# Layer kernel: the small tiles' pool ahead of the weights' pool, and a turn of seven buffers over two rings in the FFNs

## Chip, cores and metric

One core of a Trainium2 chip runs the whole kernel. The metric is the device time of one execution in microseconds, the median of three runs; lower is better. Engines: TensorE (PE in the profile; PEld is its weight load), VectorE (DVE), ScalarE (ACT), GpSimd (POOL) and SyncE (SP), which issues most of the DMAs.

## The reference

One layer of a streaming encoder on a batch of 1 with T = 256 tokens of width D = 2048, all in f32. What matters here are its two feed-forward networks (FFN1 and FFN2), with F = 5632:

```python
def swiglu(h, w_gate, w_up, w_down):
    return (jax.nn.silu(h @ w_gate) * (h @ w_up)) @ w_down

x = x + 0.5 * swiglu(rms_norm(x, ffn1_norm[i]), ffn1_w_gate[i], ffn1_w_up[i], ffn1_w_down[i])
...
x = x + mixed @ w_out[i]
x = x + 0.5 * swiglu(rms_norm(x, ffn2_norm[i]), ffn2_w_gate[i], ffn2_w_up[i], ffn2_w_down[i])
gate = jax.nn.sigmoid(rms_norm(x, ple_norm[i]) @ w_ple_gate[i])
e = (p[i] @ w_ple_proj[i]) * gate
x = x + rms_norm(e, ple_post_norm[i])
```

Between the two FFNs stands the mix (an S5 state-space group and a stick-breaking attention group with a common input and output projection); the last three lines are the last stage, the per-layer embedding.

## The kernel before

**Split matmuls.** TensorE multiplies in a rounded 32-bit format. So that the result keeps its precision, each 128x1024 half of a weight tile (two blocks of 128 rows, 512 columns) is split by `split` into hi, a rounded copy that ScalarE casts (L181), and lo, the rest, which VectorE subtracts (L184). Activations are split in the same way (nhi/nlo for a norm's output, hhi/hlo for the hidden layer and for sums). A product takes three matmuls of 128x512: hi·hi, hi·lo and lo·hi; the moving operand is the weight, the stationary one the activation. The lines are L305, L306 and L310 in `gemm_half`, and L480, L481 and L483 in `Seven.product`.

**Two ways through an FFN.** F is walked in NF = 11 column blocks of 512 for gate and up, then the down projection goes over four column blocks of D, two at a time. In blocks 0 to 6 of FFN1, beside which the preparation of S5 runs, and in block 0 of FFN2, the plain routines `gemm_block` and `gemm_pair` do the work. From block 7 of FFN1 (`early = 7`), from block 1 of FFN2 and in both down projections class `Seven` does it: some groups of four row blocks go as a `chunk`, in which sums and differences of weight blocks (VectorE, L487, tiles named sum) and of activations replace eight block products by seven, and the others as plain `column`s. A chunk calls `product` in the order 1, 5, 6, 4, 7, 2, 3.

**Where the split halves lie.** Pool `wts` has a ring of 5 for the raw weights (8,192 B per partition) and rings of 4 for whi and wlo (4,096 B each). Columns, `gemm_block`, `gemm_pair` and products 1, 2 and 3 take their halves from those. Products 5, 6, 4 and 7, made from sums, have a pool of their own, that of the phase `sums1` or `sums2`, with rings of 3 for shi and slo (beside 2 for the sums). Phases are pools that are opened and closed as the kernel goes on; they lie behind the fixed pools const, wts, act (split activations), com and small. Small holds 10 tiles of 32 B, thus 320 B per partition; wts, act and com are each a multiple of 2,048 B.

**The last stage.** `gemm_resident` multiplies with one code over three kinds of tiles: for the first quarters of the weight its halves lie in tiles of their own in a phase's pool (argument `own`), for the others in whi and wlo of wts; the stationary side is nhi/nlo (act), and for the small projection of the embedding pT, a tile of a phase's pool.

**What sets the order.** The code is written in one sequence; the framework orders each engine's instructions from it by its own estimate of what is ready, and a buffer of a ring can be written again when its last reader is done. `put_off` and `step` set where evictions and transposes stand. The raw weights are loaded on SP's queue, 1 MB a tile.

Of the kernel before, what the change touches and what calls it, by code (L numbers as in the profile page):

```python
# [2 lines left out]

# [7 lines left out]
F32R = mybir.dt.float32r  # L11
# [5 lines left out]
P = 128  # L17
# [9 lines left out]
NB = 512  # L27
# [6 lines left out]
def layer_kernel(ctx: ExitStack, tc: tile.TileContext, a: dict, shapes: dict, out: bass.AP):  # L34
# [15 lines left out]
    assert TT == 2 and NP == 64 and HC == 16 and DH == P and NC == 64 and SW == NH * DH  # L50

    cpool = ctx.enter_context(tc.tile_pool(name="const", bufs=1))
    wp = ctx.enter_context(tc.tile_pool(name="wts", bufs=4))
    actp = ctx.enter_context(tc.tile_pool(name="act", bufs=1))
    comp = ctx.enter_context(tc.tile_pool(name="com", bufs=1))
    smp = ctx.enter_context(tc.tile_pool(name="small", bufs=10))
    dramp = ctx.enter_context(tc.tile_pool(name="scratch", bufs=1, space=bass.MemoryType.DRAM))
    accp = ctx.enter_context(tc.tile_pool(name="acc", bufs=4, space=bass.MemoryType.PSUM))
    auxp = ctx.enter_context(tc.tile_pool(name="aux", bufs=2, space=bass.MemoryType.PSUM))
# [3 lines left out]
    def uid(s):  # L63
        count[0] += 1
        return f"{s}_{count[0]}"
# [7 lines left out]
    def phase(name):  # L73
        return tc.tile_pool(name=name, bufs=1, reuse_waits="tile")
# [24 lines left out]
    def step():  # L99
        for g in list(beside):  # L100
            if next(g, beside) is beside:
                beside.remove(g)

    def finish(g):
        for _ in g:
            pass
# [71 lines left out]
    def split(hi, lo, src, scale=None, pinned=False):  # L178

        if scale is None:  # L180
            copy = nc.scalar.copy(hi, src)  # L181
            if pinned:
                pin(copy)
            nc.vector.tensor_tensor(out=lo, in0=src, in1=hi.bitcast(F32), op=ALU.subtract)  # L184
        else:
            split_each(hi.unsqueeze(1), lo.unsqueeze(1), src.unsqueeze(1), [scale])
# [63 lines left out]
    def first_quarters(w, xn):  # L250
# [28 lines left out]
        xn.parted(1, second.rearrange("p (j s) -> p j s", j=4))  # L279
        return [(h, *parts[h]) for h in range(2)], weight_split(raws[1], 4)  # L280

    def weight_split(raw, nk, own=None):
        for h in range(nk // 2):
            if own:
                hi, lo = (own.tile([P, 2, NB], F32R, name=uid(s)) for s in ("whi", "wlo"))
            else:
                hi, lo = (wp.tile([P, 2, NB], F32R, tag=s, name=uid(s)) for s in ("whi", "wlo"))
            split(hi, lo, raw[:, 2 * h : 2 * h + 2, :])
            yield h, hi, lo

# [141 lines left out]
    def sum_forms(pool, u, kind="n"):  # L432

        sums = pool.tile([P, 2, NB], F32, tag="sum", name=uid("rows"), bufs=2)
        s = sums.rearrange("p j n -> p (j n)").rearrange("p (z j x b) -> p z j x b", z=4, j=2, b=32)
        (a11, a21), (a12, a22) = ([u[:, k : k + 2, 4 * t : 4 * t + 4] for t in range(TT)] for k in (0, 2))
        for z, (x, y, op) in enumerate((
            (a21, a22, ALU.subtract), (s[:, 0], a11, ALU.subtract),
            (a11, a21, ALU.subtract), (a12, s[:, 1], ALU.add),
        )):  # L440
            nc.vector.tensor_tensor(out=s[:, z], in0=x, in1=y, op=op)
        both = halves(kind)
        split(*both, sums.rearrange("p j n -> p (j n)").rearrange("p (z t) -> p z t", z=4))
        return both

    class Seven:
# [20 lines left out]
            self.begun.add(z)  # L467
            return fresh

        def product(self, z, left, src, own, final):  # L470
            hi, lo = (
                (self.pool if own else wp).tile([P, 2, NB], F32R, tag=s, name=uid(s), bufs=3 if own else None)
                for s in (("shi", "slo") if own else ("whi", "wlo"))
            )
            split(hi, lo, src)
            ps = self.bank(z)
            begin = self.begin(z)
            lh, ll = left
            for j in range(2):
                nc.tensor.matmul(ps, lhsT=lh[j], rhs=hi[:, j], start=begin and j == 0, stop=False)  # L480
                nc.tensor.matmul(ps, lhsT=ll[j], rhs=hi[:, j], start=False, stop=False)  # L481
            for j in range(2):
                nc.tensor.matmul(ps, lhsT=lh[j], rhs=lo[:, j], start=False, stop=z in final and j == 1)  # L483
# [6 lines left out]
        def chunk(self, kb, final=()):  # L490

            raws = []
            for w, n0 in self.ws:
                raw = wp.tile([P, 4, NB], F32, tag="raw", name=uid("raw"), bufs=5)
                nc.sync.dma_start(
                    raw, w[4 * kb * P : 4 * (kb + 1) * P, n0 : n0 + NB].rearrange("(j p) n -> p j n", p=P)
                )
                raws.append(raw)
            b11, b21, b12, b22 = (raw[:, 2 * h : 2 * h + 2, :] for raw in raws for h in range(2))
            parts, sums = self.act(kb), self.sums(kb)  # L500

            def whole(k, t):
                return [[u[:, 2 * k + j, t * P : (t + 1) * P] for j in range(2)] for u in parts]

            def summed(z):
                return [[u[:, z, j * P : (j + 1) * P] for j in range(2)] for u in sums]

            self.product(1, whole(0, 0), b11, False, final)
            t1 = self.add(b11, b12)
            self.product(5, summed(0), t1, True, final)  # L510
            step()
            t2 = self.add(t1, b22)
            self.product(6, summed(1), t2, True, final)
            t4 = self.add(t2, b21)
            self.product(4, whole(1, 1), t4, True, final)
            step()
            t3 = self.add(b12, b22)
            self.product(7, summed(2), t3, True, final)
            self.product(2, whole(1, 0), b21, False, final)
            step()  # L520
            self.product(3, summed(3), b22, False, final)
            step()

        def column(self, side, kbs, final=False):
# [14 lines left out]
    def ffn(i, xn, nxt, bg=None):  # L539
        wg, wu, wd = (a[f"ffn{i}_w_{s}"][0] for s in ("gate", "up", "down"))  # L540
        hT = []
        pools = ExitStack()
        early = 7 if bg else 0
        sevens = None if bg else pools.enter_context(phase(f"sums{i}"))
        hp = pools.enter_context(phase(f"h{i}"))
        side = ExitStack()
        prep = bg(side) if bg else None
# [15 lines left out]
        for f in range(NF):  # L563
            if prep and f == early:
                finish(prep)
                side.close()
                prep = None
                sevens = pools.enter_context(phase(f"sums{i}"))
                hp = pools.enter_context(phase(f"h{i}b"))
                sums = [sum_forms(sevens, whole_rows(sevens, xn(kb)), "h") for kb in range(2)]  # L570
            if sevens and f:
# [17 lines left out]
                s = Seven(xn, lambda kb: sums[kb], ((wg, f * NB), (wu, f * NB)), sevens)  # L589
# [32 lines left out]
            if f == 0 and not bg:  # L622
                both = gemm_pair(xn, ((wg, 0), (wu, 0)), KD)
                pg = next(both)
                sums = [sum_forms(sevens, whole_rows(sevens, xn(kb))) for kb in range(2)]
# [51 lines left out]
        for n in range(0, ND, 2):  # L677
# [14 lines left out]
            s = Seven(kept, lambda kb: sum_forms(sevens, rows(kb)), ((wd, n * NB), (wd, (n + 1) * NB)), sevens)  # L692
            plan = plans[n // 2]
            left = sum(u[0] == "s" for u in plan)
            for u in plan:
                kb, final = int(u[1:]), u == plan[-1]
# [715 lines left out]
    pool = s5p.enter_context(phase("s5"))  # L1412
# [10 lines left out]
    pool = atp.enter_context(phase("attn"))  # L1423
# [93 lines left out]
    s = small(1)  # L1517
# [144 lines left out]
```

## Time and profile before

| | |
|---|---|
| median of 3 runs | 1852.08 us (1851.85 to 1852.86) |
| the profiled execution | 1852.7 us, span 1850.6 us |
| TensorE busy | 1838.3 us, granted clock 1.0 |
| VectorE busy | 1460.6 us |
| ScalarE busy | 1027.4 us |
| GpSimd busy | 63.3 us |
| HBM read | 373.46 MB |

All of these but the median are of the one profiled execution. Its stages begin at (us): FFN1's blocks 0 to 6 at 0, blocks 7 to 10 at 316.29, FFN1's down projection near 478, the mix at 724.40, FFN2's block 0 near 1035, its blocks 1 to 10 at 1089.91, its down projection at 1506.75, the last stage at 1742.38. Stage by stage, the busy time of PE, PEld, DVE, ACT and POOL in windows cut near such times:

```profile
116.00:294.00 178.00, 178.00 (x1026) 146.46 (x1025) 115.62 (x127) 74.83 (x84) 21.78 (x41) 1.00 0.81 253
478.00:724.20 246.20, 245.88 (x1081) 202.29 (x1081) 196.25 (x197) 141.32 (x158) 2.52 (x4) 1.00 0.61 209
724.20:1035.00 310.80, 309.35 (x2080) 260.09 (x2079) 218.07 (x271) 191.07 (x249) 25.96 (x32) 1.00 0.62 204
1506.70:1742.20 235.50, 235.50 (x1039) 194.69 (x1039) 188.21 (x190) 137.46 (x152) 0.00 (x0) 1.00 0.62 210
```

The columns are the window, its length, the busy time of the five engines with the number of instructions, the granted clock, the DMA share and GB/s. In a row of the timeline stand the start, the duration, the engine, line and operation, what it writes and reads, and in brackets idle time just before it with the instruction that ended it. TensorE overlaps matmuls: the distance from one start to the next, and not the duration, says what one costs.

### The profile page before, as it was taken

What the parts mean: (1) busy time and instruction counts of PE and PEld (TensorE: products, weight loads), DVE (VectorE), ACT (ScalarE), POOL (GpSimd) and SP (SyncE); (2) the same over time, 40 slices, a digit from 0 to 9 for tenths busy, and PEclk for the clock granted to TensorE, in tenths of its full rate; (3) what the DMA queues carried; (4) which work ended last, traced back from release to release, by engine and by line L of the source; (5) the groups of instructions that cost most, each with busy time, mean ns of one, the idle gap of its engine ahead of it and who ended that gap; (6) DMA issues with size and microseconds to landing.
All of it is one profiled execution on the core that took longest, in us unless ns stands there. A gap on an engine that the chain in (4) does not pass through costs nothing.

```text
span 1850.6 us, 23946 instructions
## 1 busy us (share of the span) xinstructions
PE 1838.3 (99%) x9032; PEld 1518.5 (82%) x9032; DVE 1460.6 (79%) x1718; ACT 1027.4 (56%) x1187; POOL 63.3 (3%) x108
## 2 busy tenths in 40 slices
PE   9999999999999999999999999999999999999998
PEld 7888888778888888888897888888888888888887
DVE  8967665998888876687567798989898978887665
ACT  7444443655564656365685565655555555565654
POOL 0011000000000000010021000000000000000000
PEclk9999999999999999999999999999999999999999
DMA  9888868566756567675646776665656675666663
GB/s 334 281 274 277 252 217 246 173 228 200 241 196 213 192 217 248 190 262 166 216 142 218 224 262 216 235 206 198 218 198 219 207 244 185 223 195 217 208 219 125
DMA packets 232307, 406.36 MB, mean 220 GB/s; under 512 B 26784, under 2 KB 50720, under 8 KB 231904
## 3 DMA queue, kind: packets, MB, share of 16 engines
q1 hardware_dynamic: 227824, 392.81, 63.8%
q0 software_dynamic: 3648, 10.62, 1.8%
q8 instruction: 70, 1.15, 0.2%
q10 hardware_dynamic: 720, 1.41, 0.2%
q14 instruction: 45, 0.37, 0.1%
HBM read 373.46 MB, written 11.93 MB: 208 GB/s over the span
## 4 chain that ended last, share of the span: by engine, by line
PE 92%; DVE 3%; DMA 2%; ACT 2%; SPq 1%; issue 1%; DVEq 0%; ACTq 0%
PE acc L305 18%; PE acc L310 18%; PE acc L306 18%; PE aux L305 7%; PE aux L306 7%; PE aux L310 7%; PE acc L480 3%; PE acc L481 2%; PE acc L483 2%; PE aux L480 2%; PE aux L483 2%; PE aux L481 2%; DVE wlo L184 1%; SPq L1170 1%; DMA raw<-in_w_in 1%
## 5 line engine op out<-in xcount | busy, mean ns | idle before, releaser
L181 ACT CAST whi<-raw 128x1024 fp32r<-128x1024 f32 x639 | 668.1, 1052 | 684.8 <-PE acc L306 388.9
L184 DVE TENSOR_TENSOR wlo<-raw,whi 128x1024 fp32r<-128x1024 f32 x639 | 772.0, 1221 | 297.9 <-ACT whi L181 295.1
L305 PE MATMUL acc<-whi,nhi 128*128 128x512 f32 x1232 | 482.9, 392 | 1.8 <-ACT whi L181 1.7
L306 PE MATMUL acc<-whi,nlo 128*128 128x512 f32 x1232 | 479.9, 390 | 0.0
L310 PE MATMUL acc<-wlo,nhi 128*128 128x512 f32 x1232 | 340.6, 389 | 0.2 <-DVE wlo L184 0.2
L305 PEld LDWEIGHTS acc<-whi,nhi 128*128 128x128 f32 x1232 | 231.5, 188 | 52.2 <-ACT whi L181 3.0
L310 PEld LDWEIGHTS acc<-wlo,nhi 128*128 128x128 f32 x1232 | 231.2, 188 | 48.8 <-DVE wlo L184 0.6
L306 PEld LDWEIGHTS acc<-whi,nlo 128*128 128x128 f32 x1232 | 231.6, 188 | 47.2
L306 PE MATMUL acc<-whi,hlo 128*128 128x512 f32 x376 | 146.4, 389 | 0.0
L305 PE MATMUL acc<-whi,hhi 128*128 128x512 f32 x376 | 146.3, 389 | 0.0
L181 ACT CAST shi<-sum 128x1024 fp32r<-128x1024 f32 x108 | 113.4, 1052 | 43.1 <-DVE sum L487 39.6
L306 PE MATMUL aux<-whi,hlo 128*128 128x512 f32 x344 | 133.8, 389 | 0.0
L305 PE MATMUL aux<-whi,hhi 128*128 128x512 f32 x344 | 133.8, 389 | 0.0
L184 DVE TENSOR_TENSOR slo<-sum,shi 128x1024 fp32r<-128x1024 f32 x108 | 130.9, 1216 | 0.6 <-ACT shi L181 0.5
L310 PE MATMUL acc<-wlo,hhi 128*128 128x512 f32 x376 | 114.6, 389 | 0.2 <-DVE wlo L184 0.2
L310 PE MATMUL aux<-wlo,hhi 128*128 128x512 f32 x344 | 106.0, 389 | 0.0
L306 PE MATMUL aux<-whi,nlo 128*128 128x512 f32 x240 | 93.4, 389 | 0.0
L305 PE MATMUL aux<-whi,nhi 128*128 128x512 f32 x240 | 93.4, 389 | 0.0
L306 PEld LDWEIGHTS acc<-whi,hlo 128*128 128x128 f32 x376 | 70.6, 188 | 15.1 <-DVE hlo L184 0.4
L310 PEld LDWEIGHTS acc<-wlo,hhi 128*128 128x128 f32 x376 | 70.5, 188 | 15.2 <-DVE wlo L184 0.6
L305 PEld LDWEIGHTS acc<-whi,hhi 128*128 128x128 f32 x376 | 70.6, 188 | 14.6
L306 PEld LDWEIGHTS aux<-whi,hlo 128*128 128x128 f32 x344 | 64.6, 188 | 13.5
(345 smaller groups left out, 2162.6 us busy)
## 6 DMA issues: line engine op xcount, KB each, us to landing
raw<-in_ffn_w_up SPq DMA_DIRECT2D x88, 1024.0 KB, 5.8
raw<-in_ffn_w_down SPq DMA_DIRECT2D x88, 1024.0 KB, 5.1
raw<-in_ffn_w_gate SPq DMA_DIRECT2D x86, 1024.0 KB, 6.2
raw<-in_w_in SPq DMA_DIRECT2D x32, 1024.0 KB, 5.7
raw<-in_w_out SPq DMA_DIRECT2D x16, 1024.0 KB, 5.3
raw<-in_w_ple_gate SPq DMA_DIRECT2D x16, 1024.0 KB, 5.1
hT<-mid SPq DMA_DIRECT2D x160, 64.0 KB, 3.5
h<-mid SPq DMA_DIRECT2D x176, 32.0 KB, 3.6
```

What stands on the lines that cost most here:

```text
L181: copy = nc.scalar.copy(hi, src)
L184: nc.vector.tensor_tensor(out=lo, in0=src, in1=hi.bitcast(F32), op=ALU.subtract)
L305: nc.tensor.matmul(ps[t], lhsT=lh, rhs=hi[:, j, cols], start=start and j == 0, stop=False)
L306: nc.tensor.matmul(ps[t], lhsT=ll, rhs=hi[:, j, cols], start=False, stop=False)
L310: nc.tensor.matmul(ps[t], lhsT=lh, rhs=lo[:, j, cols], start=False, stop=stop and j == 1)
L480: nc.tensor.matmul(ps, lhsT=lh[j], rhs=hi[:, j], start=begin and j == 0, stop=False)
L481: nc.tensor.matmul(ps, lhsT=ll[j], rhs=hi[:, j], start=False, stop=False)
L483: nc.tensor.matmul(ps, lhsT=lh[j], rhs=lo[:, j], start=False, stop=z in final and j == 1)
L1170: nc.sync.dma_start(zt[0][p1 : p1 + HC, z], sv[p0 : p0 + HC, r % 2 * 2 + r // 2])
```

## The change

Two edits. The pool small is made ahead of wts, so every tile of wts, act and com moves up by 320 B, and the phases' tiles stay where they were. And a new function `weight_pair` hands out the buffers for each split half: while a phase made by `sums_phase` is open, it counts the halves, and of every seven the second, fourth and sixth go to that phase's shi and slo (three deep), the others to whi and wlo of wts (four deep), whether they belong to a column, to `gemm_pair` or to a product. `product` loses its argument `own`, so a half's place no longer depends on whether it was made from a sum. Outside such a phase all halves take whi and wlo, as before. The loops, the number of matmuls, casts and subtractions and the arithmetic are the same.

```diff
@@ -50,10 +50,10 @@
     assert TT == 2 and NP == 64 and HC == 16 and DH == P and NC == 64 and SW == NH * DH
 
     cpool = ctx.enter_context(tc.tile_pool(name="const", bufs=1))
+    smp = ctx.enter_context(tc.tile_pool(name="small", bufs=10))
     wp = ctx.enter_context(tc.tile_pool(name="wts", bufs=4))
     actp = ctx.enter_context(tc.tile_pool(name="act", bufs=1))
     comp = ctx.enter_context(tc.tile_pool(name="com", bufs=1))
-    smp = ctx.enter_context(tc.tile_pool(name="small", bufs=10))
     dramp = ctx.enter_context(tc.tile_pool(name="scratch", bufs=1, space=bass.MemoryType.DRAM))
     accp = ctx.enter_context(tc.tile_pool(name="acc", bufs=4, space=bass.MemoryType.PSUM))
     auxp = ctx.enter_context(tc.tile_pool(name="aux", bufs=2, space=bass.MemoryType.PSUM))
@@ -279,12 +279,30 @@
         xn.parted(1, second.rearrange("p (j s) -> p j s", j=4))
         return [(h, *parts[h]) for h in range(2)], weight_split(raws[1], 4)
 
+    ring = [None, 0]
+
+    def weight_pair():
+
+        extra, i = ring
+        ring[1] += 1
+        pool, tags = (extra, ("shi", "slo")) if extra and i % 7 % 2 else (wp, ("whi", "wlo"))
+        return [
+            pool.tile([P, 2, NB], F32R, tag=s, name=uid(s), bufs=3 if pool is extra else None) for s in tags
+        ]
+
+    @contextmanager
+    def sums_phase(name):
+        with phase(name) as pool:
+            ring[:] = [pool, 0]
+            yield pool
+            ring[0] = None
+
     def weight_split(raw, nk, own=None):
         for h in range(nk // 2):
             if own:
                 hi, lo = (own.tile([P, 2, NB], F32R, name=uid(s)) for s in ("whi", "wlo"))
             else:
-                hi, lo = (wp.tile([P, 2, NB], F32R, tag=s, name=uid(s)) for s in ("whi", "wlo"))
+                hi, lo = weight_pair()
             split(hi, lo, raw[:, 2 * h : 2 * h + 2, :])
             yield h, hi, lo
 
@@ -467,11 +485,8 @@
             self.begun.add(z)
             return fresh
 
-        def product(self, z, left, src, own, final):
-            hi, lo = (
-                (self.pool if own else wp).tile([P, 2, NB], F32R, tag=s, name=uid(s), bufs=3 if own else None)
-                for s in (("shi", "slo") if own else ("whi", "wlo"))
-            )
+        def product(self, z, left, src, final):
+            hi, lo = weight_pair()
             split(hi, lo, src)
             ps = self.bank(z)
             begin = self.begin(z)
@@ -505,20 +520,20 @@
             def summed(z):
                 return [[u[:, z, j * P : (j + 1) * P] for j in range(2)] for u in sums]
 
-            self.product(1, whole(0, 0), b11, False, final)
+            self.product(1, whole(0, 0), b11, final)
             t1 = self.add(b11, b12)
-            self.product(5, summed(0), t1, True, final)
+            self.product(5, summed(0), t1, final)
             step()
             t2 = self.add(t1, b22)
-            self.product(6, summed(1), t2, True, final)
+            self.product(6, summed(1), t2, final)
             t4 = self.add(t2, b21)
-            self.product(4, whole(1, 1), t4, True, final)
+            self.product(4, whole(1, 1), t4, final)
             step()
             t3 = self.add(b12, b22)
-            self.product(7, summed(2), t3, True, final)
-            self.product(2, whole(1, 0), b21, False, final)
+            self.product(7, summed(2), t3, final)
+            self.product(2, whole(1, 0), b21, final)
             step()
-            self.product(3, summed(3), b22, False, final)
+            self.product(3, summed(3), b22, final)
             step()
 
         def column(self, side, kbs, final=False):
@@ -541,7 +556,7 @@
         hT = []
         pools = ExitStack()
         early = 7 if bg else 0
-        sevens = None if bg else pools.enter_context(phase(f"sums{i}"))
+        sevens = None if bg else pools.enter_context(sums_phase(f"sums{i}"))
         hp = pools.enter_context(phase(f"h{i}"))
         side = ExitStack()
         prep = bg(side) if bg else None
@@ -565,7 +580,7 @@
                 finish(prep)
                 side.close()
                 prep = None
-                sevens = pools.enter_context(phase(f"sums{i}"))
+                sevens = pools.enter_context(sums_phase(f"sums{i}"))
                 hp = pools.enter_context(phase(f"h{i}b"))
                 sums = [sum_forms(sevens, whole_rows(sevens, xn(kb)), "h") for kb in range(2)]
             if sevens and f:
```

The order within the queues changes in FFN1 from block 7 on and in FFN2. VectorE at the end of FFN1's block 6 and the start of block 7, before (wlo_448 and wlo_450 are the two halves of the first weight tile of block 7, wlo_455 and wlo_457 those of the second; h and mid are block 6's result, whole and rows make the sums of activations):

```order
L184 TENSOR_TENSOR wlo_448_2846<-raw_446_2843,whi_447_2845 128x1024
L184 TENSOR_TENSOR wlo_450_2850<-raw_446_2843,whi_449_2849 128x1024
L641 SCALAR_TENSOR_TENSOR h_435_2791<-acc_411_2625,sm_74_459,sg_410_2622 128x512
L641 SCALAR_TENSOR_TENSOR h_435_2791<-acc_412_2626,sm_74_459,sg_410_2622 128x512
L216 STREAM_TRANSPOSE mid_458_2901<-h_435_2791 128x4x4x32 x2
L184 TENSOR_TENSOR wlo_455_2882<-raw_453_2879,whi_454_2881 128x1024
L184 TENSOR_TENSOR wlo_457_2886<-raw_453_2879,whi_456_2885 128x1024
L426 TENSOR_TENSOR whole_436_2819<-nhi_16_143,nlo_17_144 128x1024
L441 TENSOR_TENSOR rows_437_2821<-whole_436_2819 128x256 x2
```

And in the changed kernel:

```order
L184 TENSOR_TENSOR wlo_448_2846<-raw_446_2843,whi_447_2845 128x1024
L656 SCALAR_TENSOR_TENSOR h_435_2791<-acc_411_2625,sm_74_459,sg_410_2622 128x512
L656 SCALAR_TENSOR_TENSOR h_435_2791<-acc_412_2626,sm_74_459,sg_410_2622 128x512
L216 STREAM_TRANSPOSE mid_458_2901<-h_435_2791 128x4x4x32 x2
L184 TENSOR_TENSOR wlo_455_2882<-raw_453_2879,whi_454_2881 128x1024
L444 TENSOR_TENSOR whole_436_2819<-nhi_16_143,nlo_17_144 128x1024
L184 TENSOR_TENSOR slo_450_2850<-raw_446_2843,shi_449_2849 128x1024
L459 TENSOR_TENSOR rows_437_2821<-whole_436_2819 128x256 x2
L459 TENSOR_TENSOR rows_437_2821<-rows_437_2821,whole_436_2819 128x256
L184 TENSOR_TENSOR slo_457_2886<-raw_453_2879,shi_456_2885 128x1024
```

The second half of the first tile, now slo_450, moved from a place ahead of h to one behind h, the transposes, wlo_455 and whole.

ScalarE in FFN2's block 9, within its second chunk, before (sum_2070 is the chunk's fourth sum, for product 7; 2073 and 2077 are the halves of its last two products, 2081 and 2083 those of the next weight tile, 2086 and 2088 those of the one behind it):

```order
L181 CAST shi_2067_11620<-sum_2066_11618 128x1024
L181 CAST whi_2081_11670<-raw_2080_11668 128x1024
L181 CAST whi_2083_11674<-raw_2080_11668 128x1024
L576 COPY sg_2051_11575<-acc_2057_11585 128x512
L181 CAST shi_2071_11633<-sum_2070_11631 128x1024
L181 CAST whi_2086_11707<-raw_2085_11705 128x1024
L181 CAST whi_2088_11711<-raw_2085_11705 128x1024
```

And in the changed kernel:

```order
L181 CAST shi_2067_11620<-sum_2066_11618 128x1024
L181 CAST shi_2073_11643<-raw_2053_11577 128x1024
L181 CAST shi_2083_11674<-raw_2080_11668 128x1024
L591 COPY sg_2051_11575<-acc_2057_11585 128x512
L181 CAST shi_2088_11711<-raw_2085_11705 128x1024
L181 CAST whi_2071_11633<-sum_2070_11631 128x1024
L181 CAST whi_2077_11657<-raw_2054_11579 128x1024
L181 CAST whi_2081_11670<-raw_2080_11668 128x1024
L181 CAST whi_2086_11707<-raw_2085_11705 128x1024
```

The cast for product 7, now whi_2071, stands behind the casts of 2073, 2083 and 2088, of which the last two belong to later weight tiles.

More of the change, by code (lines that the diff above doesn't have):

```diff
@@ L1 @@
 import math
-from contextlib import ExitStack
+from contextlib import ExitStack, contextmanager
 import concourse.bass as bass
```

## The prediction

> **What bounds the kernel now.** First the page: how busy the engines are, and the tenths of the span.
>
> ```profile
> PE 1838.3 (99%) x9032; PEld 1518.5 (82%) x9032; DVE 1460.6 (79%) x1718; ACT 1027.4 (56%) x1187; POOL 63.3 (3%) x108
> PE   9999999999999999999999999999999999999998
> PEclk9999999999999999999999999999999999999999
> ```
>
> TensorE is busy from end to end at the full granted clock, so only what holds up a matmul, or stretches it, can be won or lost. To see how much that is I took the start of the first matmul of each stage from the timeline of PE, and counted the program's matmuls between (the program has 8,536; the page's x9032 counts f32 ones several times). These rows begin: the up projection of FFN1's column block 6; block 7; the mix; FFN2's block 1; FFN2's down projection; and the last stage.
>
> ```profile
> 294.53 0.39 PE L305 MATMUL acc<-whi,nhi 128*128 128x512 f32 x1
> 316.29 0.39 PE L305 MATMUL acc<-whi,nhi 128*128 128x512 f32 x1
> 724.40 0.39 PE L305 MATMUL acc<-whi,nhi 128*128 128x512 f32 x1
> 1089.91 0.39 PE L480 MATMUL acc<-whi,hhi 128*128 128x512 f32 x1
> 1506.75 0.39 PE L305 MATMUL acc<-whi,hhi 128*128 128x512 f32 x1
> 1742.38 0.39 PE L305 MATMUL acc<-whi,nhi 128*128 128x512 f32 x1
> ```
>
> Between the first two lie 96 matmuls: 21.76 us, 226.7 ns from start to start (226.65 over longer quiet stretches). I call this the normal pitch. Where the change reaches: 316.29 to 724.40 has 1,770 matmuls, 408.11 us against 401.17 at the normal pitch, 6.94 over. FFN2's up part has 1,830: 416.84 against 414.77, 2.07 over. Its down part has 1,038: 235.63 against 235.26, 0.37 over. The mix keeps its order on every engine and is left out; FFN2's block 0, which lies between, runs at the normal pitch. So **9.4 us is all there is to win**, 0.5% of the time.
>
> Next, what the 9.4 us are. The timeline of PE shows the stops of FFN1.
>
> ```profile
> 336.29 0.62 PE L483 MATMUL acc<-slo,hhi 128*128 128x512 f32 x2
> 337.80 0.50 PE L480 MATMUL aux<-shi,hhi 128*128 128x512 f32 x1 [0.89 <-ACT shi L181]
> 338.15 0.39 PE L481 MATMUL aux<-shi,hlo 128*128 128x512 f32 x1
> ...
> 364.67 0.40 PE L481 MATMUL aux<-whi,hlo 128*128 128x512 f32 x1
> 366.04 0.50 PE L480 MATMUL acc<-shi,nhi 128*128 128x512 f32 x1 [0.97 <-ACT shi L181]
> 366.37 0.39 PE L481 MATMUL acc<-shi,nlo 128*128 128x512 f32 x1
> ...
> 407.28 0.62 PE L483 MATMUL aux<-wlo,hhi 128*128 128x512 f32 x2
> 409.56 0.50 PE L480 MATMUL acc<-shi,nhi 128*128 128x512 f32 x1 [1.67 <-ACT shi L181]
> 409.90 0.39 PE L481 MATMUL acc<-shi,nlo 128*128 128x512 f32 x1
> ...
> 632.72 0.40 PE L481 MATMUL aux<-shi,nlo 128*128 128x512 f32 x1
> 633.26 0.74 PE L483 MATMUL aux<-slo,nhi 128*128 128x512 f32 x2
> 633.84 0.39 PE L480 MATMUL acc<-whi,hhi 128*128 128x512 f32 x1
> ...
> 647.49 0.39 PE L305 MATMUL acc<-whi,hhi 128*128 128x512 f32 x1
> ...
> 649.59 0.39 PE L305 MATMUL acc<-whi,hhi 128*128 128x512 f32 x1
> ```
>
> A row of x2 has its second start a pitch later. The first three stops are steps that exceed the pitch by 1.2, 1.25 and 1.95 us (for the last: 407.51 to 409.90 is 2.39, two pitches are 0.45): **4.4 us**. The two below, in the down projection, are 0.44 and, over the six matmuls from 647.49 to 649.59, 0.74 us: **1.2 us**. FFN2 has only two steps of a tenth each. That leaves 9.38 − 4.36 − 1.18 − 0.23 = **3.6 us that are no stop at all**: matmuls a few ns too long, spread over the chunks. What these are, the last stage shows most cleanly, where one routine with one code runs over three kinds of tiles:
>
> ```profile
> 1813.29 0.40 PE L305 MATMUL acc<-whi,pT 128*128 128x512 f32 x1
> 1816.09 0.40 PE L305 MATMUL acc<-whi,nhi 128*128 128x512 f32 x1
> 1821.60 0.39 PE L305 MATMUL acc<-whi,nhi 128*128 128x512 f32 x1
> 1822.97 0.39 PE L305 MATMUL acc<-whi,nhi 128*128 128x512 f32 x1
> 1827.05 0.39 PE L305 MATMUL acc<-whi,pT 128*128 128x512 f32 x1
> ```
>
> Twelve matmuls whose stationary side (pT) lies in a phase's pool and whose moving side lies in the weights' pool: 2.80 us, 233.3 ns each. Then 24 with the moving side in the phase's pool and the stationary one in the activations' pool: 5.51 us, 229.6. Then both back in the old pools: the first six take 228.3 each, the next 18 take 4.08 us, 226.7. Instructions, types and shapes are the same: what differs is **where the tiles lie**. shi and slo lie in a phase's pool too, and in before every chunk goes back and forth.
>
> **What the change does to that.** Every pool between the weights' pool and the phases is a multiple of 2,048 B per partition but one: the small pool, 320 B. Before, a weights' or activations' tile and a phase's tile are therefore never a multiple of 2,048 B apart, always 320 B off; with the small pool in front of both, they always are. If the offset makes the matmuls long, the 3.6 us go, and some 0.2 in the last stage (24 × 3.0 ns, 12 × 6.7 ns, and six at 1.7): **−3.8 us**. If it is something else, nothing goes, or more comes (rivals). The two ends are thus −3.8 and a loss; I take −3.8, since the slow rows are all such 320 B pairs, or stand right behind one, and no steady pair at one residue is slow. Against it stands the row at 1827.05, from where on both sides lie in the phase's pool, at no offset: its first six matmuls again take 228 to 236 ns, no more than the six that also follow a return to normal. This is a reading of addresses against durations, not a thing that the trace shows by itself.
>
> *By the Trainium skill* ("TensorE: Matmul & The Clock Gate", section "Step-by-step: what each phase is for") TensorE has two independent read ports into SBUF, one for the streamed side and one for the weight load, and a load takes nothing from a running matmul. By that rule the place of one side against the other cannot matter and this term is 0; the steps of 229.6 and 233.3 against 226.7 ns do not agree with it.
>
> **The turn of seven.** It adds no instruction to VectorE, ScalarE or TensorE: the same casts and subtractions write other buffers. What it changes is which buffer must be free first, and so what may stand early in an engine's queue. A row of the waits (line waited for, us in total, times, longest), two windows, and VectorE's timeline at the start of block 7:
>
> ```profile
> ACT whi L181 <- PE acc L306: 388.9, 272, 3.0
> 316.30:478.00 161.70, 158.18 (x691) 129.24 (x690) 155.02 (x159) 90.56 (x94) 4.40 (x8) 1.00 0.65 213
> 1090.00:1506.70 416.70, 416.70 (x1831) 343.23 (x1830) 375.73 (x366) 228.57 (x236) 4.33 (x8) 1.00 0.66 216
> 316.27 1.41 DVE L641 SCALAR_TENSOR_TENSOR h<-acc,sm,sg 128x512 f32<-128x512 f32 x2 [3.81 <-PE acc L310]
> 317.59 1.30 DVE L216 STREAM_TRANSPOSE mid<-h 128x512 f32<-128x512 f32 x2
> 318.81 2.32 DVE L184 TENSOR_TENSOR wlo<-raw,whi 128x1024 fp32r<-128x1024 f32 x2
> 321.05 1.22 DVE L426 TENSOR_TENSOR whole<-nhi,nlo 128x1024 f32<-128x1024 f32 x1
> 322.30 0.76 DVE L441 TENSOR_TENSOR rows<-whole 128x256 f32<-128x256 f32 x2
> ```
>
> (The windows' columns are: length, then PE, PEld, DVE, ACT, POOL busy.) ScalarE waits 388.9 us for a buffer that PE releases, so a deeper ring does let it run ahead. But in FFN1's blocks 7 to 10 VectorE is busy 155.0 of 161.7 us, and its idle time lies ahead of 316.27: a deeper ring hides nothing that VectorE hasn't done. I went through both orders and gave each VectorE row its duration from such rows (1.13 us from start to start for 128x1024). Before, wlo_450 comes ahead of block 6's h, so it is there when PE needs it; now slo_450 stands behind two h rows, two transposes, wlo_455 and whole. In the rows above that is 316.27 to 318.81, plus 1.12, plus 1.25: it begins at 321.2 and ends near 322.3, while PE, at its pace of before, wants it 16 matmuls after 316.29, at 319.9. That is a **new stop of some 2.4 us** at 320, where there was none. Behind it VectorE's sum of work is the same, and the tally gives 3.3 to 3.7 us late by 340, and no more later, against 4.36 in three stops. I take **0** for blocks 7 to 10 (from −0.7, which the tally gives, to +1). If VectorE really had slack there, up to −4.4.
>
> FFN1's down projection: the two places are late because VectorE stands still shortly before, for lack of a free buffer, and then has too much at once.
>
> ```profile
> 613.77 1.23 DVE L184 TENSOR_TENSOR wlo<-raw,whi 128x1024 fp32r<-128x1024 f32 x1 [1.49 <-ACT whi L181]
> 616.49 1.23 DVE L184 TENSOR_TENSOR wlo<-raw,whi 128x1024 fp32r<-128x1024 f32 x1 [1.49 <-ACT whi L181]
> ```
>
> The turn lets it use those 3 us, more than the 1.2 that it is late: **−1.1**.
>
> FFN2's up part has 41 us of free VectorE time (375.7 of 416.7) and no stop, so it can only lose. In block 9 the order of ScalarE, shown with the change, puts shi_2088, for a later half, ahead of whi_2071, the next product's. shi_2088's buffer is released by the matmul that starts here:
>
> ```profile
> 1385.72 0.39 PE L481 MATMUL acc<-shi,hlo 128*128 128x512 f32 x1
> L181 ACT CAST shi<-sum 128x1024 fp32r<-128x1024 f32 x108 | 113.4, 1052 | 43.1 <-DVE sum L487 39.6 <-PE acc L481 2.7 <-issue 0.3
> ```
>
> whi_2071 is wanted 9 matmuls, 2.04 us, later; the matmul's own 0.39 and two casts of 1.05 make 2.49: **+0.45**. Behind it stand the casts of two later products, with 40 matmuls of room. A place like it on VectorE in block 10 (a wlo behind the h rows and transposes) comes to +0.6 by the same count. Together **+1.0** (0 to 1.3).
>
> Moving the small pool costs no instruction. On SP's queue the weight loads move up by some rows; S5's first load at the end of FFN1 now waits for a later matmul, but the weight load behind it waits for the same one as before: 0.
>
> **Sum**: −3.8 + 0 − 1.1 + 1.0 = −3.9 us. The profiled execution took 1852.7 us (1850.6 of it the span, 2.1 around it), 0.6 above the median of 1852.08, within the 1851.85 to 1852.86 of the runs; its parts are no different, so I take the sum off the median: **1848.2 us**, own range 1845.6 to 1850.5. A difference under 0.2% (3.7 us, so 1848.4 to 1855.8) counts here as no change: the forecast lies on that edge.
>
> **Rivals.**
>
> *A phase's pool is slow in itself* (slower). Its tiles lie behind all others, and if distance or place is what costs, the change spreads the cost: 4,878 matmuls stand in FFN phases (1,770 and 3,108), three of seven halves would take 229.6 ns and the other four, each right behind such a one, 228.3: 2,091 × 3.0 ns + 2,787 × 1.7 ns = 6.2 + 4.7 us. Less the 3.6 there now and the 0.1 of the turn: +7.2, **1859.3** (1856 to 1863). For it: the six at 1827.05, and that pT is slow too. Against it: 320 B separates the cases as well. It decides wherever shi and slo matmuls stay above 229 ns.
>
> *The place of a tile within 2,048 B is what costs*, and the phases' place is the bad one: then all 7,764 matmuls of split weights move to it, 7,764 × 3.0 = 23 us less 3.7: about **1871**. For it the same six; against it, that the weights' place would have been the good one by accident.
>
> *No effect of addresses at all* (no change): the long steps come from changing tiles of any sort. The sum is then −0.1, **1852.0** (1850.5 to 1853.5). This is also what the skill's rule would give. Against it: the 18 matmuls from 1822.97 change the weights' tile every six as well, at 226.7.
>
> *All stops go as well*: 9.4 + 0.2, **1842.5**, if VectorE's order were better than I read it; little speaks for it.
>
> **Chances.** Offset 0.60 (of that 0.35 below 1848.4); no effect 0.12; phase pool slow 0.18; place within 2,048 B 0.08; all stops gone 0.02. Faster 0.37, same 0.35, slower 0.28 (0.26 from the two, the rest from larger new stops). The range, 1845.6 to 1861.0, holds the forecast's own, the case of no effect and the better part of the slow pool.
>
> **What would show it.** Right: shi and slo rows of L480 at the pitch of 226.7 in FFN2; the 24 and the 12 matmuls of the last stage too; a stop near 320 us; none at 632 and 647; small ones in FFN2's blocks 9 and 10. Wrong: shi or slo at 229 or more (the pool), every matmul longer (the place), or stops of FFN1 gone by more than 1 us.

## The result and the profile after

| | before | changed |
|---|---|---|
| median | 1851.97 us (1851.40 to 1852.86, 22 runs) | 1849.71 us (1848.78 to 1850.29, 22 runs) |
| profiled execution's span | 1850.6 us | 1848.5 us |
| ratio | 1 | 0.9987 (95% interval 0.9981 to 0.9993) |

The change is 2.3 us faster, 0.13%. That is under the 0.2% that the prediction counts as a change, yet the interval lies clear of 1. Both profiled executions took 0.6 to 0.7 us more than these medians (1852.7 and 1850.29 us), so differences between the two profiles can be compared. The first row of the page and four windows, cut at the stages' first matmuls less a quarter of a microsecond (FFN1's blocks 7 to 10, its down projection, FFN2's blocks 1 to 10, its down projection; columns as before):

```profile
PE 1836.6 (99%) x9032; PEld 1519.8 (82%) x9032; DVE 1462.7 (79%) x1718; ACT 1019.6 (55%) x1187; POOL 62.1 (3%) x108
316.20:477.81 161.61, 159.17 (x691) 130.38 (x690) 156.44 (x157) 84.69 (x89) 4.38 (x8) 0.99 0.63 211
477.81:723.76 245.95, 245.12 (x1081) 202.75 (x1080) 197.44 (x200) 142.80 (x159) 0.00 (x0) 1.00 0.61 209
1089.39:1505.71 416.32, 415.81 (x1831) 343.13 (x1830) 378.89 (x368) 228.32 (x239) 4.33 (x8) 1.00 0.65 217
1505.71:1740.99 235.28, 235.28 (x1039) 194.93 (x1038) 187.06 (x189) 133.98 (x150) 0.00 (x0) 1.00 0.61 210
```

From first matmul to first matmul the four stages took 161.77, 246.34, 416.84 and 235.63 us before: every one is shorter, by 0.2 to 0.5 us. Those are small differences of larger ones. I took the steps from start to start of all 7,764 matmuls of split weights in each trace, and divided what exceeds 226.65 ns into **long matmuls** (steps under 0.3 us) and **stops** (the others; matmuls at half clock, further down, count among them). This table, in us, also has the experiments below; "long" is the sum over the FFN stages from 316 us on, with FFN2's block 0. Long matmuls and stops are from one profiled execution of each kernel, the median is of all its runs.

| kernel | long | stops, blocks 7 to 10 | stops, FFN1 down | stops, FFN2 | median |
|---|---|---|---|---|---|
| before | 3.64 | 4.36 | 1.16 | 0.23 | 1851.97 |
| changed | 0.60 | 4.90 | 1.10 | 1.36 | 1849.71 |
| e1, small pool in front only | 0.42 | 4.49 | 0.72 | 0.41 | 1848.83 |
| e2, turn of seven only | 17.41 | 4.59 | 0.00 | 1.08 | 1866.04 |
| e3, 512 B off | 0.60 | 4.97 | 0.49 | 1.33 | 1849.44 |
| e4, turn starts at 6 | 1.04 | 3.98 | 0.00 | 2.26 | 1849.43 |
| e5, best of both | 0.49 | 4.01 | 0.00 | 0.41 | 1847.42 |
| e6, 128 B off | 15.67 | 4.49 | 0.22 | 1.07 | 1864.89 |
| e7, 448 B off | 18.22 | 4.50 | 0.11 | 1.08 | 1867.06 |
| e8, small pool between | 28.97 | 4.14 | 0.00 | 0.22 | 1892.71 |
| e9, 256 B off | 0.65 | 4.88 | 0.53 | 1.33 | 1849.68 |
| e10, 64 B off | 17.42 | 4.59 | 0.52 | 1.07 | 1865.55 |

Between before and changed, the long matmuls fell by 3.0 us and the stops grew by 1.6. The last stage shows the long ones best, at the same instructions as in the prediction (PE's timeline of the changed kernel: first the twelve with pT, then both kinds of weights' tiles, then pT again):

```profile
1811.95 0.39 PE L323 MATMUL acc<-whi,pT 128*128 128x512 f32 x1
1814.67 0.39 PE L323 MATMUL acc<-whi,nhi 128*128 128x512 f32 x1
1825.55 0.39 PE L323 MATMUL acc<-whi,pT 128*128 128x512 f32 x1
```

The twelve take 2.72 us, 226.7 ns each instead of 233.3; the next 48, of both kinds, 10.88 us, 226.7 each. Where the tiles lie no longer tells.

The stop at 320 us came as forecast. PE's timeline, and VectorE's ahead of it:

```profile
319.83 0.39 PE L324 MATMUL acc<-shi,nlo 128*128 128x512 f32 x1
322.46 0.73 PE L328 MATMUL acc<-slo,nhi 128*128 128x512 f32 x2 [2.24 <-DVE slo L184]
...
323.99 0.63 PE L324 MATMUL acc<-shi,nlo 128*128 128x512 f32 x1
324.41 1.06 PE L328 MATMUL acc<-slo,nhi 128*128 128x512 f32 x2
325.26 0.63 PE L323 MATMUL acc<-whi,nhi 128*128 128x512 f32 x1
```

```profile
316.41 1.41 DVE L656 SCALAR_TENSOR_TENSOR h<-acc,sm,sg 128x512 f32<-128x512 f32 x2 [6.54 <-PE acc L328]
317.73 1.30 DVE L216 STREAM_TRANSPOSE mid<-h 128x512 f32<-128x512 f32 x2
318.95 1.18 DVE L184 TENSOR_TENSOR wlo<-raw,whi 128x1024 fp32r<-128x1024 f32 x1
320.06 1.22 DVE L444 TENSOR_TENSOR whole<-nhi,nlo 128x1024 f32<-128x1024 f32 x1
321.19 1.22 DVE L184 TENSOR_TENSOR slo<-raw,shi 128x1024 fp32r<-128x1024 f32 x1
```

slo begins at 321.19 behind just the rows that the order put ahead of it, and the step is 2.63 us, 2.40 over the pitch. Not forecast is what follows: the steps from 323.99 on are 0.42 to 0.43 us, half speed, until 326.6. A window over it has the granted clock in its third column from the right:

```profile
323.00:326.70 3.70, 3.70 (x11) 2.88 (x10) 3.70 (x6) 1.78 (x2) 0.00 (x0) 0.55 0.86 284
```

The second thing not forecast lies at the end of FFN1's down projection. PE, then ScalarE and SP's queue:

```profile
713.19 0.50 PE L324 MATMUL aux<-whi,hlo 128*128 128x512 f32 x1 [0.83 <-DVE hlo L184]
```

```profile
703.55 1.06 ACT L181 CAST shi<-raw 128x1024 fp32r<-128x1024 f32 x1 [0.72 <-PE aux L324]
709.69 1.05 ACT L181 CAST whi<-raw 128x1024 fp32r<-128x1024 f32 x1 [5.08 <-DMA raw<-in_w_in]
710.64 1.05 ACT L181 CAST hhi<-hT 128x1024 fp32r<-128x1024 f32 x1
```

```profile
694.38 8.91 SPq L229 DMA_DIRECT2D h<-mid  x12
703.39 0.53 SPq L313 DMA_DIRECT2D raw<-in_w_in  x1
```

The cast of the mix's first weight (in_w_in) now stands ahead of an hhi that FFN1 still needs. Its load was issued at 703.39, behind twelve DMAs that turn blocks, and landed six microseconds later. The kernel before issued it later still, at 705.76, but there no cast that waited for it stood in front of an hhi. ScalarE waited 5.1 us with hhi behind; hlo and the matmul came 1.1 us late. The two old stops of the down projection, at 632 and 647, have gone.

FFN2's stops are the two that were forecast, in block 9 and block 10:

```profile
1386.58 0.51 PE L495 MATMUL aux<-whi,nhi 128*128 128x512 f32 x1 [0.30 <-ACT whi L181]
...
1474.98 0.73 PE L328 MATMUL acc<-wlo,hhi 128*128 128x512 f32 x2 [0.21 <-DVE wlo L184]
```

### The profile page after: what moved, and what is told of

Its sections match the earlier page's. It is cut to its first block, busy times and chain, and to the rows that moved or that the text cites. A ratio compares the mean times of both kernels' runs of the same rounds, so it can differ in the third digit from the quotient of the medians.

```text
span 1848.5 us, 23966 instructions
## 1 busy us (share of the span) xinstructions
PE 1836.6 (99%) x9032; PEld 1519.8 (82%) x9032; DVE 1462.7 (79%) x1718; ACT 1019.6 (55%) x1187; POOL 62.1 (3%) x108
## 5 line engine op out<-in xcount | busy, mean ns | idle before, releaser
L184 DVE TENSOR_TENSOR wlo<-raw,whi 128x1024 fp32r<-128x1024 f32 x473 | 573.2, 1224 | 214.1 <-ACT whi L181 206.5
L181 ACT CAST whi<-raw 128x1024 fp32r<-128x1024 f32 x473 | 491.4, 1050 | 398.3 <-PE acc L324 258.0
L184 DVE TENSOR_TENSOR slo<-raw,shi 128x1024 fp32r<-128x1024 f32 x166 | 202.5, 1220 | 43.8 <-ACT shi L181 43.6
L181 ACT CAST shi<-raw 128x1024 fp32r<-128x1024 f32 x166 | 174.3, 1051 | 113.4 <-PE acc L324 32.7
L181 ACT CAST whi<-sum 128x1024 fp32r<-128x1024 f32 x61 | 64.2, 1052 | 96.1 <-DVE sum L502 80.8
L181 ACT CAST shi<-sum 128x1024 fp32r<-128x1024 f32 x47 | 49.5, 1052 | 74.4 <-DVE sum L502 62.4
L324 PE MATMUL acc<-whi,hlo 128*128 128x512 f32 x216 | 84.1, 389 | 0.0
L184 DVE TENSOR_TENSOR wlo<-sum,whi 128x1024 fp32r<-128x1024 f32 x61 | 74.6, 1222 | 1.9 <-ACT whi L181 1.2
L184 DVE TENSOR_TENSOR hlo<-hT,hhi 128x1024 fp32r<-128x1024 f32 x56 | 68.3, 1219 | 4.8 <-ACT hhi L181 4.5
L502 DVE TENSOR_TENSOR sum<-sum,raw 128x1024 f32<-128x1024 f32 x54 | 66.0, 1222 | 1.0
```

Source lines behind the costliest of these rows:

```text
L324: nc.tensor.matmul(ps[t], lhsT=ll, rhs=hi[:, j, cols], start=False, stop=False)
L502: nc.vector.tensor_tensor(out=t, in0=x, in1=y, op=ALU.add)
```

## The experiments

**The two edits apart.** e1 is the kernel before with this alone:

```diff
+    smp = ctx.enter_context(tc.tile_pool(name="small", bufs=10))
     wp = ctx.enter_context(tc.tile_pool(name="wts", bufs=4))
     actp = ctx.enter_context(tc.tile_pool(name="act", bufs=1))
     comp = ctx.enter_context(tc.tile_pool(name="com", bufs=1))
-    smp = ctx.enter_context(tc.tile_pool(name="small", bufs=10))
```

> Before with the small pool in front of the weights' pool and nothing else; every engine's order is that of before. Offset theory (matmuls are long when their two operands do not lie a multiple of 2,048 B apart, as by the 320 B of before): the 3.6 us of long matmuls in the FFN stages fall to about 0.6 as in the changed kernel, the stops stay at 4.4 + 1.2 us, the time is 3.2 to 3.6 us under before, near 1848.6. Rival (the turn of seven itself took the long matmuls away): nothing changes, 1852.0.

Measured: 1848.83 us, ratio 0.9983 (0.9974 to 0.9991). Long matmuls 3.64 to 0.42 with every engine's order unchanged. So the addresses did it, and the turn had no part in it.

e2 is the changed kernel with that line moved back behind com.

> The turn of seven alone, the small pool left behind the weights' pool; every engine's order is that of the changed kernel. Offset theory: three of seven halves of 4,878 matmuls lie 320 B off and run near 229.6 ns, the halves behind them near 228.3, some 8 to 11 us of long matmuls in the FFN stages: 1857 to 1861. Rival (the turn took the long matmuls away): as the changed kernel, 1849.7.

Measured: 1866.04 us, ratio 1.0074 (1.0061 to 1.0087): 14 us slower than before, and slower than either time expected. Long matmuls are 17.4 us where 8 to 11 were expected, because halves in the weights' ring, which lie at no offset, run as long as the others: 230.1 ns from start to start in the FFN stages, against 230.5 for shi and slo. The groups by form of e2, and of the changed kernel, in which the order is the same (count, busy us and mean ns of one; here the duration, which grows with the step):

```profile
L323 PE MATMUL acc<-whi,hhi 128*128 128x512 f32 x216 | 85.2, 395 | 0.0
L323 PE MATMUL acc<-shi,hhi 128*128 128x512 f32 x160 | 63.1, 394 | 0.0
```

```profile
L323 PE MATMUL acc<-whi,hhi 128*128 128x512 f32 x216 | 84.1, 389 | 0.0
L323 PE MATMUL acc<-shi,hhi 128*128 128x512 f32 x160 | 62.3, 389 | 0.0
```

**Is it the pair of operands?** e8 is the kernel before with the small pool between the weights' and the activations' pool. Now a plain matmul's two sides are always 320 B apart, and never change; shi and slo against activations are 0 apart.

```diff
     wp = ctx.enter_context(tc.tile_pool(name="wts", bufs=4))
+    smp = ctx.enter_context(tc.tile_pool(name="small", bufs=10))
     actp = ctx.enter_context(tc.tile_pool(name="act", bufs=1))
     comp = ctx.enter_context(tc.tile_pool(name="com", bufs=1))
-    smp = ctx.enter_context(tc.tile_pool(name="small", bufs=10))
```

> The kernel before with the small pool between the weights' and the activations' pool: every plain matmul has its moving side 320 B off its stationary one, all the time, while the chunks' shi and slo against activations are 0 off. Offset theory (the pair of moving and stationary side counts): some 7,000 matmuls at 229.6 to 233.3 ns instead of 226.65, 21 to 47 us more: 1873 to 1899; shi and slo rows the shorter ones. Rival (only the change from one place of the moving side to another costs, whatever the stationary one's): as before, 1852.

Measured: 1892.71 us, ratio 1.0218 (1.0204 to 1.0232), 40 us slower, within the 21 to 47 expected (the long matmuls outside the FFN stages of the table add some 17 us). The 96 matmuls of FFN1's block 6, up, with one routine and no change of pools, have these ends in e8's timeline:

```profile
302.56 0.40 PE L305 MATMUL acc<-whi,nhi 128*128 128x512 f32 x1
...
324.95 0.40 PE L305 MATMUL acc<-whi,nhi 128*128 128x512 f32 x1
```

22.39 us, 233.3 ns each, where before they took 21.76. And the groups change sides. First e8's by form, then those of the kernel before:

```profile
L305 PE MATMUL acc<-whi,hhi 128*128 128x512 f32 x376 | 148.1, 394 | 0.0
L480 PE MATMUL acc<-shi,hhi 128*128 128x512 f32 x54 | 21.0, 389 | 0.0
```

```profile
L305 PE MATMUL acc<-whi,hhi 128*128 128x512 f32 x376 | 146.3, 389 | 0.0
L480 PE MATMUL acc<-shi,hhi 128*128 128x512 f32 x54 | 21.3, 394 | 0.0
```

The same shi tiles at the same place in the phases' pool are now the short ones and whi the long ones. From start to start in these FFN stages, halves in the weights' ring take 233.3 ns and shi and slo 227.8, against 227.0 and 229.8 before. So what counts is neither a place of its own nor the change from tile to tile alone, but where the moving side lies against the stationary one.

**Which offset counts?** Four kernels keep the changed kernel's order on every engine and move some bytes of constants from the front to behind com, or split the small pool's place.

```diff
+    tailp = ctx.enter_context(tc.tile_pool(name="tail", bufs=1))
...
-    ones = cpool.tile([P, P], F32, name="ones")
+    ones = tailp.tile([P, P], F32, name="ones")
```

That is e3, 512 B off. e6 moves rho4 in its place (128 B), e7 rho4 and the small pool (448 B).

> The changed kernel with one 512 B constant (ones) moved from the front to a pool behind com, so that phase tiles and weights' tiles are 512 B off instead of 0 mod 2,048. If 512 B or a divisor of it is the unit that counts: as the changed kernel, 1849.7, long matmuls 0.6 us. If only a multiple of 2,048 B (one row of 512 f32) is harmless: long matmuls as in the turn alone, 8 to 11 us, 1857 to 1861.

> The changed kernel with a 128 B constant (rho4) moved behind com, so phase tiles and weights' tiles are 128 B off. If 128 B or a divisor is the unit, no long matmuls: 1849.7. If 512 or 256 B is the unit: long matmuls in the FFN stages, 8 to 18 us, 1857 to 1866.

> The changed kernel with the small pool and rho4 behind com, 448 B off, which is 64 B short of 512. If the unit is 128, 256 or 512 B: long matmuls again, as in the turn alone, 1857 to 1868. If the size of the offset counts and not its rest (the 320 B are special): other than either, near 1849.7 if 64 B is the unit, which the 320 B already speak against.

Measured: e3 1849.44 us, ratio 0.9986 (0.9977 to 0.9995), as the changed kernel; e6 1864.89, ratio 1.0067 (1.0053 to 1.0081); e7 1867.06, ratio 1.0080 (1.0066 to 1.0093). So 2,048 is too strict and 128 not enough. e9 and e10 make the small pool 8 tiles deep instead of 10, and use the 64 B left over for an offset:

```diff
+    spare = ctx.enter_context(tc.tile_pool(name="spare", bufs=1)).tile([P, 16], F32, name="spare")
     wp = ctx.enter_context(tc.tile_pool(name="wts", bufs=4))
...
     comp = ctx.enter_context(tc.tile_pool(name="com", bufs=1))
+    smp = ctx.enter_context(tc.tile_pool(name="small", bufs=8))
```

This is e9, 256 B off; e10 has the two lines the other way round, 64 B off.

> The changed kernel with phase tiles and weights' tiles 256 B off: the small pool (8 tiles instead of 10) behind com, 64 B unused in front; every engine's order is that of the changed kernel. If 512 B is the unit: long matmuls in all FFN stages, 12 to 15 us, 1861 to 1867. If 256 B is: 1849.7.

> The same with the phase tiles 64 B off: the small pool (8 tiles) in front, 64 B unused behind com. If any offset that is no multiple of the unit costs alike: 1861 to 1867. If the price grows with the distance from the nearest multiple (128 B off cost 12.5 us of long matmuls where the turn at 320 B cost 14.6 over the same stages): less than at 128 B, 1853 to 1861.

Measured: e9 1849.68 us, ratio 0.9987 (0.9977 to 0.9996), long matmuls 0.65: 256 B off is as good as 0. e10 1865.55, ratio 1.0071 (1.0054 to 1.0088): 64 B off costs as much as 320. Of the offsets tried, 0, 256 and 512 are harmless and 64, 128, 320 and 448 are not, as with a period of 256 B. The two kinds of halves say the same: by that period 64 and 320 leave the same rest, and e10 and e2 agree in both (230.1 ns for halves in the weights' ring and 230.5 for shi and slo, in each), while 128 and 448 share the price otherwise (227.9 and 232.5 in e6, 228.2 and 233.3 in e7). The price does not grow with the distance from a multiple of 256: 128 B, the farthest, has 15.67 us of long matmuls, 64 B 17.42. Why halves at no offset are long at all beside others, and less so in e6 and e7, no run here tells.

**The stop at 320.** e4 starts the count at 6, so that the first two halves of block 7 both take the weights' ring:

```diff
-            ring[:] = [pool, 0]
+            ring[:] = [pool, 6]
```

> The changed kernel with the count of the turn started at 6 instead of 0, so that the first two halves of block 7 both take the weights' ring and wlo_450 stands ahead of block 6's h again. Theory (the stop at 320 us is the place of slo_450 in VectorE's queue, and the half clock behind it follows from the stop): no stop of over 0.5 us at 320, granted clock 1.0 there, stops of blocks 7 to 10 together 3.3 to 3.7 us instead of 4.9, time 1848.2 to 1848.6. Rival (VectorE's sum of work sets it, the lateness only moves): the stops add up to 4 us or more further on, time near 1849.5.

Measured: 1849.43 us, ratio 0.9985 (0.9976 to 0.9994). The stop at 320 and the half clock are gone, but most of it comes back some 20 us later (e4's timeline of PE):

```profile
336.84 0.50 PE L495 MATMUL aux<-whi,hhi 128*128 128x512 f32 x1 [1.39 <-ACT whi L181]
...
341.63 0.50 PE L498 MATMUL acc<-slo,nhi 128*128 128x512 f32 x1 [0.52 <-DVE slo L184]
```

Blocks 7 to 10 stop for 3.98 us in all, not 3.3 to 3.7. So 0.9 of the 4.90 us went with the order of the start, and 4.0 stayed, which speaks for the rival: VectorE's sum of work sets it, and the order only places it. The start at 6 moves other rows too, so this is argued and not shown by e4 alone. e9 says the same from the other side. It has the changed kernel's order and the same stop, but no half clock behind it:

```profile
322.46 0.73 PE L329 MATMUL acc<-slo,nhi 128*128 128x512 f32 x2 [2.24 <-DVE slo L185]
...
324.40 0.39 PE L324 MATMUL acc<-whi,nhi 128*128 128x512 f32 x1
...
325.76 0.39 PE L324 MATMUL acc<-whi,nhi 128*128 128x512 f32 x1
...
342.96 0.50 PE L496 MATMUL aux<-shi,hhi 128*128 128x512 f32 x1 [0.98 <-ACT shi L182]
```

The six matmuls from 324.40 take 1.36 us, 226.7 ns each. At 343 it stops once more, idle for 0.98 us, where the changed kernel has no idle time; blocks 7 to 10 stop for 4.88 us, against 4.90 with the half clock. What the clock took, PE would have waited for anyway. The kernels 64 to 448 B off agree: 4.59 us with the half clock (e2, e10), 4.49 and 4.50 without (e6, e7).

The down projection has no stop at all in e4. ScalarE's timeline there:

```profile
705.63 1.05 ACT L181 CAST hhi<-hT 128x1024 fp32r<-128x1024 f32 x1 [2.12 <-PE aux L328]
709.00 1.71 ACT L191 ACTIVATE nhi<-h,gains 128x256 fp32r<-128x256 f32 x4 [2.31 <-DMA h<-mid]
```

hhi is cast at 705.63, with no cast of the mix ahead of it, while the load of in_w_in went out 1.4 us earlier than in the changed kernel. So the stop at 713 comes with that cast. But its place alone is not enough: e2 has the order of the changed kernel on every engine, the cast in the same place, and no stop in the down projection. Its row of ScalarE:

```profile
714.14 1.05 ACT L181 CAST whi<-raw 128x1024 fp32r<-128x1024 f32 x1 [3.97 <-DMA raw<-in_w_in]
```

Seven kernels have this order. ScalarE's wait for the load and the stops of the down projection are, in us: e2 3.97 and 0.00, e7 4.25 and 0.11, e6 4.31 and 0.22, e3 4.47 and 0.49, e9 4.50 and 0.53, e10 4.65 and 0.52, the changed kernel 5.08 and 1.10. Some 4 us of waiting cost nothing here; the later the load comes beyond that, the longer PE stops, by about as much. Why the start at 6 moves the cast I have not traced. FFN2, where the count starts at 6 too, is worse with it (2.26 us).

**A version that beats both.** e5 has the small pool in front, the turn from 6 in FFN1 alone, and FFN2's halves where the kernel before had them.

```diff
+        if old is not None:
+            extra, i = (old, 1) if own else (None, 0)
...
-            ring[:] = [pool, 0]
+            ring[:] = [pool, 6, None] if name == "sums1" else [None, 0, pool]
...
-            hi, lo = weight_pair()
+            hi, lo = weight_pair(z in (5, 6, 4, 7))
```

> Small pool in front, the turn of seven in FFN1 alone (its count started at 6), FFN2 with the halves where the kernel before had them. By the stages of the runs so far: FFN1's blocks 7 to 10 160.7 us and its down projection 244.8 as with the start at 6, FFN2 as with the small pool alone (415.3 and 235.3): 1.1 us under the small pool alone, 1847.7. Rival (the shorter FFN1 stages depend on what FFN2's queues take, or SP's queue returns the wait at FFN1's end): 1848.5 to 1849.

Measured: 1847.42 us, ratio 0.9974 (0.9965 to 0.9984). That is 4.6 to 4.9 us under the kernel before, and it came by the stages: 160.67 and 244.80 us in FFN1, 415.28 and 235.36 in FFN2.

## Why the prediction was right, and where not

The direction, and 1848.2 us for 1849.7, came from the right mechanism. Of −3.9 us in the sum, −2.3 came. The time alone does not show that, since 1849.7 lies but 0.8 us outside the range given to the rival of no effect; the steps of the matmuls and the experiments do. Term by term, in the profiled executions:

- **Offset of the pools, −3.8.** Measured −3.0 in the FFN stages (3.64 to 0.60) and −0.44 in the last stage, together −3.5. Shown by e1 alone and by e8. The last stage brought more than the 0.2 counted, because 24 further matmuls with pT, from 1785.90 us on, also took 233.3 ns before and 226.7 after (0.16 us). The unit was wrong: 2,048 B is too strict, 256 B is enough; at no offset that made no difference. Of the 0.4 to 1.0 us left in the kernels at a harmless offset a part are the matmuls behind a stop, which are long in every kernel; I did not follow the rest.
- **FFN1's blocks 7 to 10, 0 (−0.7 to +1).** Measured +0.5. The new stop was forecast at 2.4 us and was 2.40. The half clock behind it was not foreseen, but by e9, e6 and e7 it cost 0.1 us at most here, since VectorE was late anyway.
- **FFN1's down projection, −1.1.** This is the step that failed: measured −0.1. In e3 and e9, with the same order and a harmless offset, the stops are 0.49 and 0.53, so −0.6 to −0.7: ScalarE waited longest for the load in the profile of the changed kernel. None of the three reaches −1.1. That the turn "lets it use those 3 us" held, since the stops at 632 and 647 are gone. But I followed only what the deeper turn frees for VectorE, not what it lets into ScalarE's queue: a cast of the next stage, whose load was late, ahead of one that was needed. I had looked at SP's queue for this very passage and called it 0, by which matmul a load waits for, without asking what is queued behind the load's first reader.
- **FFN2, +1.0.** Measured +1.1, with 0.6 at 1386 and 0.5 at 1475, the two places named, and the rest in smaller steps beside them, less the 0.2 of before.
- Elsewhere: up to block 6 of FFN1 +0.15 us, mix and FFN2's block 0 +0.1, and behind the last split matmul −0.5, none of which I explain.

−3.48 + 0.54 − 0.06 + 1.13 = −1.87, and −0.24 from elsewhere: −2.1, the difference of the spans.

The rivals. A slow phase pool and a bad place within 2,048 B both fall with the changed kernel itself, in which shi and slo run at 389 ns as whi does, and with e8. No effect of addresses falls with e1. The six long matmuls from 1827.05 in the kernel before, at no offset, stay open in part. They took 224 to 236 ns, 230.3 on average, so somewhat more than the 228.3 of the six that the prediction set beside them. In the changed kernel the same ones, from 1825.55 on, are short, so that the place of their own tiles is not it, but why a change of both sides at once to another rest lengthens the first few, no run here tells. The rates in the slow-pool rival, 229.6 and 228.3 ns, were too low for a stream that changes every six matmuls: in e2 the FFN stages ran at 230.1 to 230.4 throughout (229.2 in FFN2's block 0).

The rule of two independent read ports, from the Trainium skill ("TensorE: Matmul & The Clock Gate", section "Step-by-step: what each phase is for"), by which a load takes nothing from a running matmul, leaves no room for what e8 shows: with one side 320 B off, the same matmuls take 233.3 instead of 226.7 ns. Which read holds up which, and why 256 B is the unit, no run here tells.

## What to carry to other kernels

Where two pools feed the two sides of matmuls such as these, keep every pool between them a multiple of 256 B per partition: here 320 B in the wrong place cost 3 us with few mixed pairs, 17 with many, and 40 with nearly all. Other types and shapes were not tried. A deeper ring that lets an engine run ahead also lets work of the next stage into its queue; ask for each such instruction when its data arrives, and what stands behind it. And try two edits apart before keeping both: one of these two was worth 3.2 us, and the other, as written, gave 0.9 of it back.

## What the hardware showed that I had not expected

- A period of 256 B in the offset of a matmul's two operands, as far as seven offsets tell: the same price for 64 and 320 B off (17.4 us of long matmuls for both), and 2.9% on each matmul where the offset is steady (233.3 against 226.7 ns).
- The half clock. All seven profiled kernels with the turn from 0 stop near 320 for 2.2 us. In four of them (changed, e2, e3, e10) some eight matmuls at 427 ns follow; in three (e6, e7, e9) none does, after a stop of the same length. Stops of 1.7 us and less, in before, e1, e4, e5 and e8, are followed by none. The Trainium skill ("TensorE: Matmul & The Clock Gate", section "HAM oscillation — how this bites in real kernels") warns of idle gaps over some 3.4 us; here an idle time of 2.2 us was enough at times, so the measurement is the stricter. What decides between the four and the three is open. The same page's "Back-to-back issue gap" gives N/1.2 ns for a matmul at half clock, 427 ns for 512 columns, and the trace agrees.
